# Moving a norm's sums to VectorE, a rescaling by one product, and a row broadcast's place in a two-block network on one core

## The chip, the cores and the metric

The kernel runs on one core of a Trainium2 chip. Its time is the device time of one execution in microseconds, the median of repeated runs. The core's engines work side by side and each takes its own instructions in the order in which the program lists them: PE (TensorE, matrix products; PEld is its weight load), DVE (VectorE), ACT (ScalarE), POOL (GpSimd) and SP, which here only issues DMAs. They wait for each other through semaphores.

## The reference

A sequence of 256 tokens with 1024 features passes two different blocks of two layers each; all is float32.

```
for i in range(2):                       # first block
    proj = rmsnorm(x, norm_mix[i]) @ w_in[i]
    q, k, v, cb, cc, cx, u, g = split(proj)
    y_attn = sliding_window_attention(rope(q), rope(k), v, sinks) @ w_attn_o[i]
    y_conv = (cb * short_conv(cc * cx, conv_w[i])) @ w_conv_o[i]
    ys = gelu(s5_ssm(u, ...));  y_ssm = (ys * sigmoid(ys @ w_ssm_glu[i])) @ w_ssm_o[i]
    x = x + (gated sum of y_attn, y_conv, y_ssm) @ w_mix_o[i]
    x = x + swiglu(rmsnorm(x, norm_ffn[i]))
x = rmsnorm(x, norm_final)
for l in range(2):                       # second block
    u = rmsnorm(h, norm_mix_w[l]) @ w_in[l]
    q, k, v, g_ret, z, xbc, dt, gate_ret, gate_ssd = split(u)
    yr = retention(rotary(q), rotary(k), v)            # 4 heads
    yr = silu(g_ret) * yr * rsqrt(mean(yr^2) + eps);   o_ret = yr @ ret_out
    xs, B, C = split(silu(conv(xbc)));  dtp = softplus(dt + dt_bias);  a = -exp(a_log)
    ys = (ssd_scan(xs * dtp, dtp * a, B, C) + d_skip * xs) * silu(z)
    ys = ys * rsqrt(mean over each of 4 groups(ys^2) + eps) * ssd_norm_w;  o_ssd = ys @ ssd_out
    h = h + (sigmoid(gate_ret) * o_ret + sigmoid(gate_ssd) * o_ssd) @ w_o
    h = h + swiglu(rmsnorm(h, norm_ffn_w[l]))
return rmsnorm(h, final_norm_w)
```

## The kernel before

Features lie on the 128 partitions and tokens along the free side: `X` holds x as 8 slices of 128 features by 256 tokens. Each product is done in three passes of fp32r matmuls: an operand is cut into a high part and the rest, and high times high, high times rest and rest times high are added. For the activations that pair is `xhl`. For weights `chunk` (line 264) does it as they stream in: a DMA on SP's queue fills `raw` (4 buffers of 128x1024), ACT copies it to `wh`, DVE subtracts to `wl` (5 buffers each). So a stream of DMA, ACT and DVE steps of one chunk each runs ahead of PE through the whole kernel. `fm` gives a product with features on the partitions, `tm` with tokens there, `fmb` is a two-pass form; `mid` hooks let other work in at half of a product. A scheduler orders each engine's instructions by the order of the code and by its own reckoning of when operands are ready; `tc.high_priority(offset=URGENT)` lets some go ahead, and `pinned` keeps a piece behind whatever its engines were given before it.

**Norms.** The scale of an rmsnorm is not known when the products that need it start. They run on `X` times the norm's gain, and the scale comes in later. While the last product of a layer ends, `Norm.pair(mp)` (line 426) makes the `xhl` of two slices and `squares(mp)` squares them on ACT into `sq` (2 buffers), and adds them into `acc`: on VectorE for the last pair and for the first norm of all, otherwise on GpSimd (line 444). `steps` sums `acc` over the partitions with four small matmuls into `st`, and takes a reciprocal square root of two columns on DVE (`rsqrt`, line 371: 15 or so tiny instructions). `rowbc` (line 398) makes a row of it for all partitions: two diagonal tiles `dg` on DVE, two small matmuls into `ax`, and a copy. `rescale` then overwrites `xhl` with the scaled values: four multiplications on POOL into `sq`, eight casts on ACT, eight subtractions on DVE.

**State space of the first block.** While layer 0 of the first block ends, and through its feed-forward, the kernel prepares the tables of layer 1's state-space model: steps A1 and A2 on POOL (powers and rotations, tiles `BP`, `W`, `g`), PC, CP, BX, WK, KK on the other engines, each pinned, in the order of `PLAN_1`.

**Retention (`layer2`).** For head 0 the products for q, k and v run on unscaled `xhl`. In the middle of v's product `mid_v` finishes the norm and rotates q and k with scaled tables; v is scaled as it leaves PSUM (line 1399), `nm.rescale()` follows (line 1402), and the product for the gate `sg` (line 1404, `silu2`) reads scaled `xhl`. Later heads need nothing of the kind. `head_tail` normalizes a head's result with `rd` (line 1355).

**State space of the second block.** Four groups follow, with three convolved products, two products for z and one gate each. What is left of a group, `group_tail` (line 1475), is a generator that `bg.tick()` moves on by one step after each product of the next group: two steps with the decay matrices, sums of squares in `acc`, one step for the next decay matrices, one with the small sum into `ax`, `rsqrt` and `dg`, one with the two matmuls on `dg` and the copy `rdb`, and a last one that makes the tiles `y`. `dt_prep` (line 1244) is run in steps between the four products with `ret_out`; it loads `a_log` into `al` and takes its exponential (line 1261).

Of the kernel before, what the change touches and what calls it, by code (L numbers as in the profile page):

```python
# [13 lines left out]
ALU = mybir.AluOpType  # L14
# [55 lines left out]
def body(ctx, tc, A, out):  # L70
# [29 lines left out]
    def axt(shape=(128, 2, 256)):  # L100
        return T(ax, list(shape), "ax")
# [7 lines left out]
    def add(o, a, b, eng=V):  # L109
        return tt(o, a, b, ALU.add, eng)  # L110
# [7 lines left out]
    def ts(o, a, s1, s2, op0, op1, eng=V):  # L118
        return eng.tensor_scalar(out=o, in0=a, scalar1=s1, scalar2=s2, op0=op0, op1=op1)

    def act(o, i, f, bias=None, scale=None, accum=None):
        kw = {}
        if bias is not None:
            kw["bias"] = bias
        if scale is not None:
            kw["scale"] = scale
        if accum is not None:
            kw["accum_out"] = accum
        return SC.activation(out=o, in_=i, func=f, **kw)  # L129
# [265 lines left out]
            stt(y, t, 1.5, src, ALU.add, ALU.mult)  # L395
        return y

    def rowbc(colv, o):

        dg = T(sqp, [128, 2, 128], "dg")  # L400
        with tc.high_priority(offset=URGENT):
            for b in range(2):
                ts(dg[:, b, :], ident, colv[:, b:b + 1], None, ALU.mult, ALU.bypass)
        yield
        ps = axt([128, 512])
        for b in range(2):
            mmu(ps[:, b * 128:b * 128 + 128], ones, dg[:, b, :], b == 0, b == 1)
        cp(o, ps[:, 0:S])
# [3 lines left out]
    class Norm:  # L412
# [24 lines left out]
        def squares(self, mp):  # L437
            sq = T(tmp, [128, 2, S], "sq")
            act(sq, X[:, 2 * mp:2 * mp + 2, :], AF.Square)
            if self.sqgain is not None:  # L440
                self.sums()
                self.todo = mp, sq
                return
            eng = V if mp == 3 or self.gain is gfirst else G
            if mp == 0:
                self.acc = T(sqp, [128, S], "acc")
                add(self.acc, sq[:, 0], sq[:, 1], eng)
            else:
                for k in range(2):
                    add(self.acc, self.acc, sq[:, k], eng)  # L450

        def sums(self):
            if self.todo is None:
# [766 lines left out]
        sub(o[:, 0, :], a[:, 0, :], b[:, 1, :])  # L1220
        add(o[:, 1, :], b[:, 0, :], a[:, 1, :])

    def silu2(ps, o):

        for b in range(2):
            act(o[:, b], ps[b], AF.Tanh, scale=0.5)
            stt(o[:, b], o[:, b], 1.0, ps[b], ALU.add, ALU.mult)

    def layer2(l, nm, nxt):
# [13 lines left out]
        def dt_prep():  # L1243
            pd = mmt()
            for k0, kn, (wh, wl) in chunks(w, 11264, D, n=32):
                for k in range(kn):
                    kt = k0 + k
                    mmu(pd[0:32, 0, :], wl[:, k, :], xh[:, kt, :], kt == 0, False)
                    mmu(pd[0:32, 0, :], wh[:, k, :], xl[:, kt, :], False, False)
                    mmu(pd[0:32, 0, :], wh[:, k, :], xh[:, kt, :], False, kt == D // 128 - 1)  # L1250
            acr = T(lp, [32, S], "acr")
            cp(acr, pd[0:32, 0, :])
            yield
            ps = axt()
            for b in range(2):
                PE.transpose(ps[:, b, 0:32], acr[:, 128 * b:128 * b + 128], ident[0:32, 0:32])
            dtb = T(lp, [128, 32], "dtb")
            nc.sync.dma_start(out=dtb, in_=A["dt_bias_2"][l].partition_broadcast(128))
            al = T(lp, [128, 32], "al")
            nc.sync.dma_start(out=al, in_=A["a_log_2"][l].partition_broadcast(128))  # L1260
            act(al, al, AF.Exp)
            x = T(lp, [128, 2, 32], "x")
            for b in range(2):
                add(x[:, b, :], ps[:, b, 0:32], dtb)
            e = T(lp, [128, 2, 32], "e")
            z_ = T(lp, [128, 2, 32], "z_")
            pl = T(lp, [128, 2, 32], "pl")
            stt(e, x, -1.0, x, ALU.mult, ALU.max)
            act(e, e, AF.Exp, scale=-1.0)
            ts(pl, e, 2.0, None, ALU.add, ALU.bypass)  # L1270
            V.reciprocal(out=pl, in_=pl)
            mul(e, e, pl)
            mul(z_, e, e)
            ts(pl, z_, 1.0 / 17.0, None, ALU.mult, ALU.bypass)
            for kk in range(7, 0, -1):
                stt(pl, pl, 1.0 / (2 * kk + 1), z_, ALU.add, ALU.mult)
            stt(pl, pl, 1.0, e, ALU.add, ALU.mult)
            ts(x, x, 0.0, None, ALU.max, ALU.bypass)
            dtp = T(lp, [128, 2, 32], "dtp")
            stt(dtp, pl, 2.0, x, ALU.mult, ALU.add)  # L1280
            la = T(lp, [128, 2, 32], "la")
            stt(la, dtp, -1.0, bc(al, 2), ALU.mult, ALU.mult)
            dth = T(lp, [128, 2, 32], "dth")
            ts(dth, dtp, 0.5, None, ALU.mult, ALU.bypass)
            yield
            pn = axt([128, 512])
            mmu(pn[:, 0:32], tri, la[:, 0, :], True, True)
            mmu(pn[:, 32:64], strict, la[:, 0, :], True, True)
            mmu(pn[:, 64:96], tri, la[:, 1, :], True, True)
            for b in range(2):  # L1290
                mmu(pn[0:32, 128 + 128 * b:256 + 128 * b], la[:, b, :], tri, True, True)
            ncol = T(lp, [128, 3, 32], "ncol")
            V.tensor_copy(out=ncol[:, 0, :], in_=pn[:, 0:32])
            ts(ncol[:, 1, :], pn[:, 32:64], -1.0, None, ALU.mult, ALU.bypass)
            V.tensor_copy(out=ncol[:, 2, :], in_=pn[:, 64:96])
            acr = T(lp, [32, S], "acr")
            cp(acr, pn[0:32, 128:384])
            acd = T(dramp, [32, S], f"acd{l}")
            nc.sync.dma_start(out=acd, in_=acr)
            sd.update(dth=dth, ncol=ncol, acd=acd)  # L1300
# [29 lines left out]
        def head_tail(h):  # L1330
            qT, kT, v, sg = (hd[h][k] for k in ("qT", "kT", "v", "sg"))
            dec = T(r1, [128, 384], "dec")
            nc.sync.dma_start(out=dec, in_=A["decay"][h])
            pst = axt([128, 512])
            for kk in range(2):
                mmu(pst[:, 0:256], kT[:, kk, 0:128], qT[:, kk, :], kk == 0, False)
            for kk in range(2):
                mmu(pst[:, 256:384], kT[:, kk, 128:256], qT[:, kk, 128:256], False, kk == 1)
            stt_ = T(r2, [128, 384], "st")
            mul(stt_, pst[:, 0:384], dec)  # L1340
            yield
            y3 = T(r2, [128, 2, 512], "y3")
            ss = T(sm, [128, 2], "ss")
            for b in range(2):
                py = axt([128, 512])
                if b == 0:
                    mmu(py, stt_[:, 0:128], v[:, 0, :], True, True)
                else:
                    mmu(py, stt_[:, 128:256], v[:, 0, :], True, False)
                    mmu(py, stt_[:, 256:384], v[:, 1, :], False, True)  # L1350
                sq = T(tmp, [128, 2, S], "sq").rearrange("p a s -> p (a s)")
                act(sq, py, AF.Square, accum=ss[:, b:b + 1])
                mul(y3[:, b], py, sg[:, b])
                yield
            rd = rsqrt(ss, 2, 1.0 / 512)
            ts(rd, rd, 0.5, None, ALU.mult, ALU.bypass)
            for b in range(2):
                ts(y3[:, b], y3[:, b], rd[:, b:b + 1], None, ALU.mult, ALU.bypass)
            yield
            for c in range(2):  # L1360
                pt = axt()
                for m in range(2):
                    for b in range(2):
                        k = (2 * c + m) * 128
                        PE.transpose(pt[:, m, 128 * b:128 * b + 128], y3[:, b, k:k + 128], ident)  # L1365
                t = pair(yp, "y")
                split(t, pt)
                yr[2 * h + c] = t
                yield

        for h in range(4):
# [26 lines left out]
            for b in range(2):  # L1398
                cp(v[:, b, :], ps[b], nm.rsc[:, b:b + 1] if h == 0 else None)
            bg.tick()  # L1400
            if h == 0:
                nm.rescale()
            sg = e["sg"] = T(r2, [128, 2, 512], "sg")
            silu2(tm(w, 4096 + 512 * h, D, XX, mid=bg.tick), sg)
            bg.tick()
            bg.add(head_tail(h))
            if h == 0 and nm.sqgain is not None:
# [66 lines left out]
        def group_tail(g):  # L1474
# [28 lines left out]
            ps = axt([128, 512])  # L1503
            for b in range(2):
                mmu(ps[:, b:b + 1], acc[:, b * 128:b * 128 + 128], ones[:, 0:1], True, True)
            rd = rsqrt(ps[:, 0:2], 2, 1.0 / 512)
            rdb = T(d1, [128, S], "rdb")
            yield from rowbc(rd, rdb)
            yield
            for c in range(2):  # L1510
                t = pair(yp, "y")
                mul(sz[c], sz[c], bc(rdb, 2))
# [139 lines left out]
```

## Time and profile before

| | |
|---|---|
| time, median of 3 runs | 2252.89 us (2251.32 to 2256.33) |
| the profiled execution's own time | 2256.99 us |
| its span, first to last instruction | 2255.2 us |
| busy PE / DVE / ACT / POOL | 97% / 69% / 54% / 9% of the span |
| mean granted clock of TensorE | 0.986 |
| moved from HBM | 386.88 MB, 175 GB/s over the span |

PE is busy nearly all the time and does the same matmuls whatever the order, so what can change is its idle time and the stretches in which it is granted half its clock. The waits in which PE stands idle are short and spread over the span, but for one of 16.94 us.

### The profile page before, as it was taken

The page shows a single profiled execution, that of the slowest core. Times are in us where ns is not written, and L with a number is a line of the kernel's source. Part 1 is how long each engine was busy: PE and PEld are TensorE (multiplying, and loading weights), DVE is VectorE, ACT ScalarE, POOL GpSimd, SP SyncE. Part 2 cuts the span into 40 slices and gives each one's busy share as a digit, 9 for nine tenths or more (in the row PEclk, how much of TensorE's full clock was granted, in tenths as well). Part 3 has the DMA queues.
Part 4 walks back from the last instruction along what each step waited for, and adds up shares of the span by engine and source line. Part 5 has one row for each costly group of instructions (what it writes and reads, how often), then busy time and mean ns, then how long its engine had stood idle before and what let it go on. Part 6 is the DMA issues. An engine that isn't in the chain of part 4 may idle for free. (4 is left out here: it accounts for less than half of the span.)

```text
span 2255.2 us, 36864 instructions
## 1 busy us (share of the span) xinstructions
PE 2178.6 (97%) x14368; PEld 1971.0 (87%) x14368; DVE 1548.2 (69%) x2515; ACT 1221.7 (54%) x1949; POOL 199.6 (9%) x359
## 2 busy tenths in 40 slices
PE   7999969999999999999999999999999999999997
PEld 6898958899999889888999989889888899989886
DVE  7766646568756655776568887556766668887554
ACT  6666537645555444444476755444444477655442
POOL 5810244001000000100000000000100000000000
PEclk9899989999999999999999999999999999999999
DMA  6443537766645655555566646555555566456553
GB/s 184 148 127 122 168 120 240 233 207 220 195 136 178 191 186 173 162 186 165 160 201 202 187 157 192 186 174 183 171 166 177 161 200 199 149 185 196 185 178 103
DMA packets 343935, 397.75 MB, mean 176 GB/s; under 512 B 27988, under 2 KB 276688, under 8 KB 342736
## 3 DMA queue, kind: packets, MB, share of 16 engines
q1 hardware_dynamic: 342816, 394.48, 56.0%
q8 instruction: 113, 1.85, 0.3%
q10 hardware_dynamic: 592, 0.79, 0.1%
q14 instruction: 62, 0.51, 0.1%
q0 software_dynamic: 352, 0.11, 0.0%
HBM read 386.88 MB, written 8.45 MB: 175 GB/s over the span
## 5 line engine op out<-in xcount | busy, mean ns | idle before, releaser
L104 DVE TENSOR_TENSOR wl<-raw,wh 128x1024 fp32r<-128x1024 f32 (+1 forms) x698 | 850.1, 1221 | 516.5 <-ACT wh L129 488.4
L129 ACT ACTIVATE wh<-raw 128x1024 fp32r<-128x1024 f32 (+1 forms) x698 | 727.8, 1047 | 822.5 <-PE mm L135 663.4
L135 PE MATMUL mm<-xhl,wh 128*128 128x256 f32 x3616 | 672.2, 287 | 4.9 <-ACT xhl L129 3.2
L135 PE MATMUL mm<-wh,xhl 128*128 128x512 f32 (+1 forms) x2176 | 645.3, 381 | 3.0 <-DVE xhl L116 1.3
L135 PEld LDWEIGHTS mm<-xhl,wh 128*128 128x128 f32 x3616 | 567.7, 192 | 11.5 <-ACT xhl L129 4.1
L135 PE MATMUL mm<-xhl,wl 128*128 128x256 f32 (+1 forms) x1808 | 515.3, 285 | 3.8 <-DVE wl L104 3.8
L135 PEld LDWEIGHTS mm<-wh,xhl 128*128 128x128 f32 x2176 | 398.7, 190 | 81.3 <-issue 4.3
L135 PE MATMUL mm<-wl,xhl 128*128 128x512 f32 (+1 forms) x1088 | 410.4, 377 | 5.5 <-DVE wl L104 5.5
L135 PEld LDWEIGHTS mm<-xhl,wl 128*128 128x128 f32 (+1 forms) x1808 | 347.6, 192 | 5.7 <-DVE wl L104 4.9
L135 PEld LDWEIGHTS mm<-wl,xhl 128*128 128x128 f32 x1088 | 206.8, 190 | 43.2 <-DVE wl L104 6.0
L135 PE MATMUL mm<-hh,wh 128*128 128x512 f32 (+1 forms) x660 | 185.4, 348 | 0.0
L135 PE MATMUL mm<-y,wh 128*128 128x512 f32 (+1 forms) x576 | 182.1, 372 | 1.0 <-DVE y L116 1.0
L135 PE MATMUL mm<-hh,wl 128*128 128x256 f32 x528 | 147.9, 280 | 0.0
L135 PE MATMUL mm<-y,wl 128*128 128x256 f32 x512 | 144.3, 282 | 0.0
L135 PEld LDWEIGHTS mm<-hh,wh 128*128 128x128 f32 x660 | 114.7, 188 | 16.7
L135 PEld LDWEIGHTS mm<-y,wh 128*128 128x128 f32 x576 | 103.8, 188 | 21.9 <-DVE y L116 1.7
L104 POOL TENSOR_TENSOR acc<-sq 128x256 f32<-128x256 f32 x6 | 4.8, 795 | 1245.3 <-ACT sq L129 1245.3
L135 PEld LDWEIGHTS mm<-hh,wl 128*128 128x128 f32 x528 | 99.1, 188 | 0.0
L135 PEld LDWEIGHTS mm<-y,wl 128*128 128x128 f32 x512 | 96.2, 188 | 0.5 <-issue 0.3
L135 PE MATMUL mm<-mg,wh 128*128 128x256 f32 x512 | 90.5, 280 | 0.0
L135 PEld LDWEIGHTS mm<-mg,wh 128*128 128x128 f32 x512 | 78.4, 189 | 0.0
L116 DVE SCALAR_TENSOR_TENSOR ta<-mm,vec,ta 128x255 f32<-128x255 f32 (+2 forms) x144 | 67.2, 476 | 9.5 <-ACT ta L129 9.2
(363 smaller groups left out, 2446.6 us busy)
## 6 DMA issues: line engine op xcount, KB each, us to landing
raw<-in_w_in_dram SPq DMA_DIRECT2D x284, 512.0 KB, 4.3
raw<-in_w_ffn_in_dram SPq DMA_DIRECT2D x88, 512.0 KB, 3.6
raw<-in_w_gate_up_dram SPq DMA_DIRECT2D x88, 512.0 KB, 3.5
raw<-in_w_down_dram SPq DMA_DIRECT2D x42, 512.0 KB, 3.8
raw<-in_w_ffn_out_dram SPq DMA_DIRECT2D x40, 512.0 KB, 3.5
raw<-in_ret_out_dram SPq DMA_DIRECT2D x32, 512.0 KB, 3.8
raw<-in_ssd_out_dram SPq DMA_DIRECT2D x32, 512.0 KB, 3.4
raw<-in_w_mix_o_dram SPq DMA_DIRECT2D x16, 512.0 KB, 3.4
```

Of the source, the lines that this page charges most:

```text
L104: return eng.tensor_tensor(out=o, in0=a, in1=b, op=op)
L116: return V.scalar_tensor_tensor(out=o, in0=a, scalar=s, in1=b, op0=op0, op1=op1)
L129: return SC.activation(out=o, in_=i, func=f, **kw)
L135: return PE.matmul(out=o, lhsT=l, rhs=r, start=start, stop=stop)
```

## The change

Three edits go together, with a pin for one exponential:

- `Norm.squares` adds all squares on VectorE; GpSimd has no part in sums any more.
- In head 0 of the retention the product for the gate runs on unscaled `xhl`. Its tanh takes the scale as an operand (`rh`, half of `nm.rsc`), the factor that is still missing in front comes in with `rd` in `head_tail`, and `nm.rescale()` is called behind the product.
- In the state-space norm `rsqrt` gets priority; `rowbc` gives back control once more between `dg` and its matmuls, and the step behind the copy goes.
- The exponential of `al` is pinned behind what ACT was given before.

```
-            eng = V if mp == 3 or self.gain is gfirst else G
             if mp == 0:
                 self.acc = T(sqp, [128, S], "acc")
-                add(self.acc, sq[:, 0], sq[:, 1], eng)
+                add(self.acc, sq[:, 0], sq[:, 1])
             else:
                 for k in range(2):
-                    add(self.acc, self.acc, sq[:, k], eng)
+                    add(self.acc, self.acc, sq[:, k])
...
-    def rowbc(colv, o):
+    def rowbc(colv, o, wait=False):
...
         yield
+        if wait:
+            yield
         ps = axt([128, 512])
...
-    def silu2(ps, o):
+    def silu2(ps, o, r=None):
         for b in range(2):
-            act(o[:, b], ps[b], AF.Tanh, scale=0.5)
+            act(o[:, b], ps[b], AF.Tanh, scale=0.5 if r is None else r[:, b:b + 1])
...
-            act(al, al, AF.Exp)
+            pinned(lambda: act(al, al, AF.Exp))
...
-            ts(rd, rd, 0.5, None, ALU.mult, ALU.bypass)
+            if h == 0:
+                stt(rd, rd, 0.5, nm.rsc, ALU.mult, ALU.mult)
+            else:
+                ts(rd, rd, 0.5, None, ALU.mult, ALU.bypass)
...
+            sg = e["sg"] = T(r2, [128, 2, 512], "sg")
+            pg = tm(w, 4096 + 512 * h, D, XX, mid=bg.tick)
             if h == 0:
+                rh = T(sm, [128, 2], "r8")
+                ts(rh, nm.rsc, 0.5, None, ALU.mult, ALU.bypass)
+                silu2(pg, sg, rh)
                 nm.rescale()
-            sg = e["sg"] = T(r2, [128, 2, 512], "sg")
-            silu2(tm(w, 4096 + 512 * h, D, XX, mid=bg.tick), sg)
+            else:
+                silu2(pg, sg)
...
-            rd = rsqrt(ps[:, 0:2], 2, 1.0 / 512)
+            with tc.high_priority(offset=URGENT):
+                rd = rsqrt(ps[:, 0:2], 2, 1.0 / 512)
             rdb = T(d1, [128, S], "rdb")
-            yield from rowbc(rd, rdb)
-            yield
+            yield from rowbc(rd, rdb, True)
```

The scheduler decides what stands where. The first place is VectorE at the end of layer 0's mixer, where `acc_3315` is the sum of the feed-forward norm's squares and `wl` are rests of weight chunks:

```order
 L116 SCALAR_TENSOR_TENSOR xhl_92<-X,vec,xhl_92 128x256 x2
+L104 TENSOR_TENSOR acc_3315<-sq_3313 128x256
 L104 TENSOR_TENSOR wl_3490<-raw_3488,wh_3489 128x1024
 L116 SCALAR_TENSOR_TENSOR X<-mm_3317,X 128x512
 L104 TENSOR_TENSOR wl_3561<-raw_3559,wh_3560 128x1024
 L116 SCALAR_TENSOR_TENSOR xhl_92<-X,vec,xhl_92 128x256 x2
+L104 TENSOR_TENSOR acc_3315<-acc_3315,sq_3383 128x256 x2
 L104 TENSOR_TENSOR wl_3579<-raw_3577,wh_3578 128x1024
 L116 SCALAR_TENSOR_TENSOR X<-mm_3387,X 128x512
 L104 TENSOR_TENSOR wl_3649<-raw_3647,wh_3648 128x1024
 L116 SCALAR_TENSOR_TENSOR xhl_92<-X,vec,xhl_92 128x256 x2
+L104 TENSOR_TENSOR acc_3315<-acc_3315,sq_3453 128x256 x2
```

The five adds of the first three pairs now stand on VectorE right behind the `xhl` of their pair; on POOL they stood between state-space steps. The last pair's two adds stay where they were.

The second place is ScalarE at head 0 of the last layer's retention, from the copy of the norm's row (`rsb`) on; `xhl` from `sq` are the casts of `rescale`. Before:

```order
L129 ACTIVATE rsb_17035<-ax_17077 128x256
L129 ACTIVATE xhl_92<-sq_17133,vec 128x256 x2
L129 ACTIVATE xhl_92<-sq_17139,vec 128x256 x2
L129 ACTIVATE wh_17215<-raw_17214 128x1024
L129 ACTIVATE v_16890<-mm_17039,rsc_17016 128x512
L129 ACTIVATE wh_17241<-raw_17240 128x1024
L129 ACTIVATE v_16890<-mm_17040,rsc_17016 128x512
L129 ACTIVATE xhl_92<-sq_17145,vec 128x256 x2
L129 ACTIVATE xhl_92<-sq_17151,vec 128x256 x2
```

And now:

```order
L129 ACTIVATE rsb_17037<-ax_17079 128x256
L129 ACTIVATE wh_17193<-raw_17192 128x1024
L129 ACTIVATE v_16892<-mm_17041,rsc_17018 128x512
L129 ACTIVATE wh_17245<-raw_17244 128x1024
L129 ACTIVATE v_16892<-mm_17042,rsc_17018 128x512
L129 ACTIVATE xhl_92<-sq_17216,vec 128x256
L129 ACTIVATE wh_17275<-raw_17274 128x1024
L129 ACTIVATE xhl_92<-sq_17216,vec 128x256
L129 ACTIVATE xhl_92<-sq_17222,vec 128x256
L129 ACTIVATE wh_17321<-raw_17320 128x1024
L129 ACTIVATE xhl_92<-sq_17222,vec 128x256
L129 ACTIVATE xhl_92<-sq_17228,vec 128x256
```

The casts stand one or two at a time between weight chunks, behind v's two copies; four of them stood ahead of those copies. The last two stand among the gate's tanh.

The third place is PE in the second block's state space, at the tail of the third group in layer 0; `dg` is the diagonal of its norm, `mm_14500` the first product with `ssd_out`. Before:

```order
L135 MATMUL mm_14348<-xhl_92,wl_14381 128x256
L135 MATMUL mm_14500<-y_13319,wh_14503 128x512
...
L135 MATMUL mm_14501<-y_13319,wh_14503 128x512
L135 MATMUL ax_14330<-dg_14264,C 128x128 x2
L1471 MATMUL ax_14335<-C,xs_2239_13886 128x128 x2
```

And now, where the gate's product is `mm_14346` and the product with `ssd_out` `mm_14502`:

```order
L135 MATMUL mm_14346<-xhl_92,wl_14379 128x256
L135 MATMUL ax_14408<-dg_14266,C 128x128 x2
L135 MATMUL ax_14425<-Lm_14143,xd_14332 64x256 x2
...
L135 MATMUL ax_14440<-Lm_14159,xd_14332 64x128 x2
L135 MATMUL mm_14502<-y_13321,wh_14505 128x512
```

Nine matmuls on `y` that stood ahead of `dg`'s now stand behind it, and the eight transposes of `xs` moved from behind `dg`'s matmuls to the start of the gate's product. In the first and second group `dg`'s matmuls stand three matmuls of the gate's product earlier than before.

## Rows read from the trace of the kernel before

**Rows 1.** The page: busy time, share of the span and instructions.

```profile
PE 2178.6 (97%) x14368; PEld 1971.0 (87%) x14368; DVE 1548.2 (69%) x2515; ACT 1221.7 (54%) x1949; POOL 199.6 (9%) x359
```

**Rows 2.** Waits of PE over the span: who waits for whom, total us, times, longest.

```profile
PE st L135 <- DVE acc L104: 16.9, 1, 16.9
...
PE ax L135 <- DVE dg L119: 8.3, 5, 3.2
...
PE mm L135 <- ACT xhl L129: 3.2, 2, 2.6
```

**Rows 3.** Timeline of PE: start, us, instruction, count, [idle before, what ended it].

```profile
307.12 1.01 PE L135 MATMUL st<-C,acc 128*128 128x1 f32 x4 [16.94 <-DVE acc L104]
...
1320.02 0.71 PE L135 MATMUL ax<-dg,C 128*128 128x128 f32 x4 [1.26 <-DVE dg L119]
...
1588.28 0.50 PE L135 MATMUL mm<-xhl,wh 128*128 128x256 f32 x2 [2.57 <-ACT xhl L129]
...
1607.86 0.47 PE L135 MATMUL mm<-wh,xhl 128*128 128x512 f32 x1 [0.43 <-DVE tb L104]
1608.74 0.49 PE L135 MATMUL mm<-wh,xhl 128*128 128x512 f32 x1 [0.41 <-ACT v L129]
1610.02 0.50 PE L135 MATMUL mm<-wh,xhl 128*128 128x512 f32 x1 [0.79 <-DVE xhl L116]
```

**Rows 4.** Timeline of POOL: a norm's last adds, and the last layer's rescaling.

```profile
304.62 1.52 POOL L104 TENSOR_TENSOR acc<-acc,sq 128x256 f32<-128x256 f32 x2
...
1602.78 3.45 POOL L104 TENSOR_TENSOR sq<-X,rsb 128x512 f32<-128x512 f32 x2 [29.18 <-issue]
```

**Rows 5.** Timeline of DVE at the end of layer 0's mixer.

```profile
281.26 0.87 DVE L116 SCALAR_TENSOR_TENSOR xhl<-X,vec,xhl 128x256 fp32r<-128x256 f32 x2
...
286.95 1.59 DVE L116 SCALAR_TENSOR_TENSOR xhl<-X,vec,xhl 128x256 fp32r<-128x256 f32 x2
306.18 0.89 DVE L104 TENSOR_TENSOR acc<-acc,sq 128x256 f32<-128x256 f32 x2 [17.64 <-POOL acc L104]
```

**Rows 6.** Stretches: us, busy PE, PEld, DVE, ACT, POOL, then clock, DMA share, GB/s.

```profile
307.10:313.25 6.15, 6.13 (x16) 4.98 (x17) 4.83 (x19) 0.13 (x1) 0.00 (x0) 0.50 0.54 167
...
952.00:958.00 6.00, 6.00 (x20) 4.75 (x20) 6.00 (x10) 2.01 (x5) 3.55 (x2) 0.72 0.16 47
...
1610.00:1616.00 6.00, 5.98 (x19) 4.79 (x20) 6.00 (x9) 1.94 (x6) 3.54 (x2) 0.72 0.13 30
...
1938.00:1942.00 4.00, 3.41 (x17) 3.42 (x17) 3.53 (x8) 1.40 (x4) 0.00 (x0) 0.57 0.85 260
...
1208.00:1236.00 28.00, 26.98 (x228) 26.41 (x225) 25.39 (x51) 23.61 (x44) 0.00 (x0) 1.00 0.56 165
```

**Rows 7.** Instructions on `acc`: count, min/median/max ns, first and last start.

```profile
L104 DVE TENSOR_TENSOR acc<-acc,sq x34: 411/418/427, 17.3 to 2057.6; 128x256 f32<-128x256 f32 x34
...
L104 POOL TENSOR_TENSOR acc<-acc,sq x24: 721/762/804, 291.3 to 2051.9; 128x256 f32<-128x256 f32 x24
```

**Rows 8.** Timeline of ACT: a square, `al`, and v in the last layer.

```profile
293.32 0.63 ACT L129 ACTIVATE sq<-X 128x512 f32<-128x512 f32 x1 [6.81 <-POOL acc L104]
...
1586.65 0.23 ACT L129 ACTIVATE al<-al 128x32 f32<-128x32 f32 x1 [4.34 <-DMA al<-in_a_log_dram]
...
1608.03 0.67 ACT L129 ACTIVATE v<-mm,rsc 128x512 f32<-128x512 f32 x1
```

**Rows 9.** Timeline of DVE: last layer's first norm and rescaling, second group's `dg`.

```profile
1583.80 0.68 DVE L104 TENSOR_TENSOR X<-X,ta 128x512 f32<-128x512 f32 x1
...
1613.91 2.71 DVE L116 SCALAR_TENSOR_TENSOR xhl<-sq,vec,xhl 128x256 fp32r<-128x256 f32 x4
...
1936.52 1.23 DVE L104 TENSOR_TENSOR wl<-raw,wh 128x1024 fp32r<-128x1024 f32 x1 [2.06 <-ACT wh L129]
...
1938.24 0.48 DVE L119 TENSOR_SCALAR dg<-C,ny 128x128 f32<-128x128 f32 x2
```

## Prediction

> **What bounds the kernel now.** I read the page's busy times first: PE is busy 97% of the span [rows 1], and the change leaves its matmuls as they are. So time can come only from PE's idle stretches and from stretches at half clock, and next come PE's waits, grouped by who ends them [rows 2]. One stands out: the statistics product `st` waits 16.9 us, once, for `acc` on VectorE. The waits for `dg` come to 8.3 us in five, and those for casts of `xhl` to 3.2 us in two. The timeline of PE then says where each lies [rows 3]; the timelines of POOL, DVE and ACT [rows 4, 5, 8, 9] say what was late, and the windows [rows 6] what the clock did afterwards. VectorE has 31% of its span free [rows 1], so extra adds there cost nothing by themselves; they cost only where PE waits for what stands behind them.
>
> **Sums on VectorE.** In the feed-forward norm of the first layer, PE is ready for `st` at 307.12 − 16.94 = 290.18. VectorE's last two adds stand idle for 17.64 us and end that wait [rows 5]; they follow POOL's two adds of 304.62, which end at 306.14 [rows 4]. Those are nothing in themselves (762 ns each, [rows 7]): they stand behind state-space steps in POOL's queue. ACT's last square was held too, 6.81 us for a buffer of `sq` [rows 8]; without that it is done at 293.32 − 6.81 + 0.63 = 287.1. In the changed kernel the adds of the first three pairs follow their `xhl` on VectorE, and the last two follow the `xhl` pair that ends at 286.95 + 1.59 = 288.54 [rows 5]. At 418 ns each [rows 7] that is 289.4, before PE's 290.18. The stall goes, and so does its aftermath: for 6.15 us behind it the granted clock is 0.50 [rows 6], the lower level, which costs 3.1 us. 16.9 + 3.1 = 20.0.
>
> Against it: that `xhl` pair took 1.59 us where the one before took 0.87 [rows 5], at a time when POOL was in its state-space steps. If the two adds are stretched as the pair was (1.83 times), they end at 290.1; if each is held a whole 0.8 us (one POOL add), at 291.0, and `st` waits 0.8 us, with as much again for what stands before. I take 0.5 us lost: **19.5** (18.4 to 20.0).
>
> The Trainium skill ("SBUF — State Buffer", section "Who interferes with whom") says that a VectorE instruction with two SBUF inputs contends with a GpSimd instruction that reads SBUF, and that the loser blocks fully. An `acc` add is such an instruction, so the rule speaks against moving adds to an engine beside a busy POOL; the 1.59 against 0.87 us agree with it. By it the term would be its lower end, 18.4, since each add can lose one POOL instruction and no more.
>
> Thirty adds move. 24 of them show as POOL's [rows 7], and 30 × 0.418 = 12.5 us of VectorE work is hidden by its idle time. At the other norms' ends no wait of PE on POOL's adds shows beside the one of 16.9 [rows 2], so nothing is gained there; where cover is gone a norm's end may cost up to 1.6 us, as above. POOL's state-space steps only come earlier.
>
> **The rescale, one product later.** In the last layer's head 0 PE has three gaps near the end of v's product: 0.43 for the tables `tb`, 0.41 for `v`, 0.79 for `xhl` [rows 3], in all 1.63; the other layer has 0.2 less. Behind them the clock averages 0.72 over 6 us in either layer [rows 6], which is 3.4 us at half clock, or 1.7 lost. Now the gate's product reads unscaled `xhl`: its 0.79 goes. v's copies (0.67, [rows 8]) stand ahead of all casts, where four stood before them, so I take the 0.41 as gone; the 0.43 for `tb` stays, since the tables come from the same norm chain. That leaves 1.2 of gaps, cut to 1.0 for the smaller layer and the tables' jitter. The clock falls after the three gaps together; with one left I give its return 0.7, 1.2 of 1.7. **2.2 a layer, 4.4 in all.** What is late next is the rescaling's end: POOL's `sq` takes 3.45 [rows 4], and VectorE's last four `xhl` end at 1616.62 [rows 9], 13.8 us behind the first multiplication. It now has to overwrite `xhl` behind the last reading matmul of the gate's product, and head 1's q product reads it next. But the overwriting goes by slices and can follow the gate's last pass slice by slice, and that product comes to its last slices some 3.6 us in (a quarter of a three-pass product at the pace seen here). From below: if 5 us of the chain show in the two layers together, the term is −0.6; if more, it is the last rival. Bounds −0.6 to 6.4 (all gaps and all the clock).
>
> **`al` pinned.** In the last layer ACT stands 4.34 us for the DMA of `al`, and its casts and weight copies stand behind; PE's first product waits 2.57 us for `xhl` [rows 8, 3]. X is ready at 1584.48 [rows 9], before al's 1586.65, so the cast had only ACT to wait for. Pinned behind what was given before, the exponential stands near `dt_prep`'s others, its data long there. **2.4** (0 to 2.57, since another link may be late by a few tenths).
>
> **The state-space norm's row.** PE waits for `dg` five times over 0.2 us, 8.3 in all, 3.2 the longest [rows 2]; 1.26 at 1320.02 is the third group of the first of the two layers [rows 3]. In groups one and two `dg` still stands behind the same `wl` on VectorE, which is 25.39 of 28 us busy there [rows 6], so it hardly comes earlier: at 1936.52 a `wl` starts late behind ACT, ends 1937.75, and `dg` starts at 1938.24 [rows 9], 0.49 that `rsqrt`'s last small instructions take. With priority these go ahead of that `wl`. But PE's `dg` matmuls come three matmuls, some 0.36 us (at 28/228, [rows 6]), earlier too. Net 0.2 to 0.9 a place, I take 0.5: 2.0 at four. The 4 us at clock 0.57 behind the long wait [rows 6] are 3.4 us at half, 1.7 lost, of which I credit 0.7: 1.2. In the third group `dg` stands two `wl` earlier, and nine matmuls on `y` that stood ahead now follow as cover at the tail: 0.7 and 0.5. **4.4.** Bounds: if PE's earlier arrival eats everything, −1; if all 8.3 and 1.7 go, and the tail's 0.5 with them, 10.5.
>
> **The sum.** 19.5 + 4.4 + 2.4 + 4.4 = 30.7. The profiled execution took 2256.99, 4.1 above the median of the runs; 2256.99 − 30.7 = 2226.3, and as a median 2226.3 − 4.1 = **2222.2**.
>
> **Rivals.**
> - *The `dg` waits stay.* Everything that `rsqrt` gains is lost to the earlier matmuls, because VectorE's queue of `wl` sets both. For it: 25.39 of 28 us busy. Against: the longest wait began behind ACT, not behind that queue. 2222.2 + 4.4 = 2226.6; 0.12.
> - *The adds on VectorE make waits of their own.* At six norm ends (those not already summed there) up to 1.6 us shows, since `xhl` and weight rests stand behind the adds. For it: the stretched pair. Against: VectorE is 31% idle. 2222.2 + 6 × 1.6 = 2231.8; 0.10.
> - *All `dg` waits go.* The term is 10.5 to 11, the time 2215.7; 0.11.
> - *The rescaling shows whole* (the other side). If POOL's multiplications, the casts and the rests cannot start before the gate's product has been read through, head 1's q product waits for the chain of 13.8 us in either layer: 27.7, and with clock loss as behind the 16.94 stall, 3.1 each, 33.8; the 4.4 of that edit is lost as well. 2222.2 + 33.8 + 4.4 = 2260.4, 0.3% slower. It decides from the point where more than 1616.62 − 1602.78 − 3.6 = 10.2 us of the chain lie behind the gate's last matmul. For it: one buffer `xhl` is read and overwritten. Against: writes go by slices, and four of the eight casts stood between v's matmuls before without harm but 0.79. 0.03.
> - *The change doesn't do what it says:* the 16.9 us come from something other than POOL's adds, ACT's square or the last `xhl`, and half of the stall stays: 2232. 0.02.
>
> **How the numbers follow.** My forecast has 0.62, with its own range 2217 to 2228. To hold eight in ten I take in the ends with dear adds and with all `dg` waits gone: **2212 to 2236**. This kernel's measurement tells about 0.2%, 4.5 us, from no change. Only the rescaling rival ends above 2257, so slower has 0.03; between 2248 and 2257 some 9 to 18 of 30.7 us would have to be lost beyond the rivals above, 0.02; faster has 0.95.
>
> **What would show it.** In the changed kernel's profile: no `st` wait for `acc` above 1 us, no `acc` rows on POOL, and a granted clock of 1.00 from 285 to 310; no gap near 1588 for `xhl`, and `al` much later on ACT; before the gate's product at most one gap, and full clock behind it; a sum of waits for `dg` of 4 to 6 us. It is wrong if head 1's q product waits for `xhl` by more than a microsecond, if feed-forward products of any norm newly wait for `acc`, or if the 20 us come back as a wait for the state-space tables of the next layer.

## The result and the profile after

The changed kernel takes 2225.34 us (median of 4 runs, 2222.40 to 2227.24), the kernel before 2254.61 (4 runs): 29.3 us less, a ratio of 0.987, 95% interval 0.9852 to 0.9889. The forecast was 2222.2, which is 30.7 us below 2252.89, the median of the kernel before that was known then. The profiled execution of the changed kernel took 2224.35, with a span of 2222.6; the mean granted clock is 0.989.

First the page's busy times, and the grouped waits of PE (total us, times, longest), as in [rows 1, 2].

```profile
PE 2171.8 (98%) x14368; PEld 1966.6 (88%) x14368; DVE 1553.1 (70%) x2547; ACT 1221.3 (55%) x1949; POOL 183.7 (8%) x329
```

```profile
PE ax L135 <- DVE dg L119: 3.1, 5, 1.8
PE mm L135 <- ACT xhl L129: 2.5, 1, 2.5
PE mm L135 <- DVE xhl L116: 1.1, 2, 0.8
```

The row of `st` is gone, that of `dg` fell from 8.3 to 3.1, and the 2.5 for casts is one wait at the start of the program. `xhl` from VectorE is still there, but its two waits are others (below). PE is busy 6.8 us less with the same matmuls: that is clock, and the rest of the gain is idle time.

Then the places of the prediction on the timeline of PE (start, us, instruction, count, idle before and what ended it):

```profile
291.81 0.50 PE L135 MATMUL st<-C,acc 128*128 128x1 f32 x4
...
1256.84 0.71 PE L135 MATMUL ax<-dg,C 128*128 128x128 f32 x4 [1.78 <-DVE dg L119]
...
1583.84 0.70 PE L135 MATMUL mm<-wh,xhl 128*128 128x512 f32 x2 [0.43 <-DVE tb L104]
...
1599.85 0.39 PE L135 MATMUL mm<-xhl,wh 128*128 128x256 f32 x1 [0.80 <-DVE xhl L116]
```

Against [rows 3]: `st` has no idle time ahead of it (16.94 before). Of the three gaps near the end of v's product the one for `tb` is left. The gap of 0.79 for `xhl` is no longer there, but one of 0.80 stands 16 us later, in head 1's q product, behind the rescaling's last rest. The gap of 2.57 at 1588 has no successor; `al` now runs at 1764.9 in that layer.

The windows answer to [rows 6] (us, busy PE, PEld, DVE, ACT, POOL, then clock, DMA share, GB/s): full clock behind the norm and around the gate's product, and half clock left at the second group's `dg` of the first of the two layers.

```profile
285.00:310.00 25.00, 25.00 (x124) 21.04 (x123) 23.56 (x39) 12.91 (x20) 23.68 (x42) 1.00 0.57 174
931.00:937.00 6.00, 5.67 (x25) 4.72 (x26) 6.00 (x11) 3.77 (x7) 0.00 (x0) 1.00 0.28 87
1584.00:1604.00 20.00, 19.20 (x114) 17.00 (x113) 18.80 (x26) 11.38 (x18) 3.87 (x2) 1.00 0.59 183
...
1257.00:1261.00 4.00, 4.00 (x22) 4.00 (x23) 2.62 (x4) 2.08 (x4) 0.00 (x0) 0.57 0.96 302
```

Where the time came from can be read by following one matmul after another through both timelines:

| PE reaches | before | after | difference |
|---|---|---|---|
| first product after attention, layer 0 of the first block | 231.88 | 233.73 | +1.9 |
| `ax<-U,W` of its layer 1 | 520.94 | 502.60 | −18.3 |
| the wait for `tb`, layer 0 of the second block | 949.57 | 931.33 | −18.2 |
| `ax<-BC` of that layer | 1174.16 | 1153.43 | −20.7 |
| the wait for `tb`, last layer | 1607.86 | 1583.84 | −24.0 |
| `ax<-BC` of the last layer | 1833.07 | 1806.35 | −26.7 |
| last matmul's end | 2243.93 | 2211.30 | −32.6 |

These are single executions, 32.6 us apart, so the steps add up to more than the 29.3 between the medians. The stretch of the sums gave 20.2, the gate's product 2.5 and 2.7, `al` and the first layer's `dg` 3.3 together, the last layer's tails 5.9. The first 1.9 are not the change's: up to there every engine runs the same instructions in the same order in both kernels, and what differs is PE's idle time (28.1 us against 26.8) and the granted clock (0.93 against 0.95).

### The profile page after: what moved, and what is told of

Its sections match the earlier page's. It is cut to its first block, busy times and chain, and to the rows that moved or that the text cites. A ratio compares the mean times of both kernels' runs of the same rounds, so it can differ in the third digit from the quotient of the medians.

```text
span 2222.6 us, 36844 instructions
## 1 busy us (share of the span) xinstructions
PE 2171.8 (98%) x14368; PEld 1966.6 (88%) x14368; DVE 1553.1 (70%) x2547; ACT 1221.3 (55%) x1949; POOL 183.7 (8%) x329
## 4 chain that ended last, share of the span: by engine, by line
PE 78%; ACT 5%; DMA 4%; DVE 4%; issue 1%; SPq 0%; POOL 0%; ACTq 0%; DVEq 0%; POOLq 0%
PE mm L135 71%; PE ax L135 5%; ACT Lm L129 2%; DMA raw<-in_w_in_dram 2%; DMA Lm<-acd 2%; ACT wh L129 1%; DVE wl L104 1%; PE ax L567 1%; ACT ta L129 0%; DVE Lm L104 0%; PE ax L1369 0%; ACT tb L129 0%; PE st L135 0%; PE ax L1480 0%; DVE ta L116 0%
## 5 line engine op out<-in xcount | busy, mean ns | idle before, releaser
L104 POOL TENSOR_TENSOR sq<-X,rsb 128x512 f32<-128x512 f32 x12 | 21.8, 1823 | 1196.0 <-ACT rsb L129 1168.6
```

The source lines that it names most:

```text
L104: return eng.tensor_tensor(out=o, in0=a, in1=b, op=op)
```

## Experiments

Each ran beside the kernel before on the same chip. Gains are worked out from the ratio and the time of before there (2256 us for the first eight), not from the two medians. The first four make one edit each on the kernel before.

**The sums alone.**

```
-            eng = V if mp == 3 or self.gain is gfirst else G
...
-                    add(self.acc, self.acc, sq[:, k], eng)
+                    add(self.acc, self.acc, sq[:, k])
```

> Only the squares' adds go to VectorE; everything else as before. Theory: the stall of 16.9 us is POOL's queue and goes whole, with the half clock behind it: 20 us, so about 2234.5 against 2254.6; the wait of st for acc under 1 us, and all that stands behind that point earlier by the same 20 us to the end of the program (within 1 us), since 12.5 us of adds on VectorE are covered everywhere else. Rival: the adds on VectorE cost at the other norms' ends; then the lead of 20 us shrinks by 1 to 1.6 us at each of up to six places, and the time is 2240 or more.

Measured: 2233.54 against 2255.98, ratio 0.9909 (0.9891 to 0.9926), 20.5 us (17 to 25). `st` starts at 292.70 with no idle time. Between the first product after attention and `ax<-U,W` this trace has 268.9 us, the changed kernel's 268.9, that of the kernel before 289.1, and no other norm's end shows a new wait for `acc`. The rival falls: the adds are covered everywhere else.

**The gate's product alone** (the part of the diff on `silu2`, `rh`, `rd` and `rescale`).

> Only the rescaling one product later in the second block. Theory: 2.5 us a layer, so 5 us, about 2249.6 against 2254.6; of the three gaps near the end of v's product the first, 0.43 for tb, stays and the other two go; the granted clock stays at 1.00 there; a gap of 0.3 to 0.8 for xhl comes back in head 1's q product. Rival: the chain of the rescaling shows at head 1's q product in full, over 5 us a layer, and the time is above 2254.6.

Measured: 2249.44, ratio 0.9981 (0.9967 to 0.9995), 4.3 us (1 to 7). The gaps for `v` and `xhl` are gone in both layers, that for `tb` stays, and head 1's q product waits 0.33 and 0.81 for `xhl`. The gain agrees with the theory's 5 us; of the rescaling's chain the last microsecond shows, not its 13.8.

**The norm's row alone** (`rsqrt`'s priority, the extra step, the last step taken away).

> Only the state-space norm's row: priority for its rsqrt, dg's matmuls a step later. Theory: 6.5 us, about 2248, of it 6 in the last layer (the wait of 3.2 with its half clock goes) and below 1 in the first (the second group's 1.8 stays). Rival 1: the first forecast, 4.4 us, 2250.2, with 0.5 at each place. Rival 2: this edit gains nothing by itself, and the last layer's gain in the changed kernel came from where the weight stream stood after the other edits; then 2254 and the wait of about 3 us stays.

Measured: 2249.69, ratio 0.9977 (0.9964 to 0.9991), 5.2 us (2 to 8). The waits for `dg` sum to 5.2. But the last layer's second group still waits 3.11: the long wait, whose end I had put down to this edit after reading the trace, stayed. Neither the theory's split nor the forecast's holds.

**`al` alone.**

> Only the exponential of al pinned. Theory: PE's gap of 2.57 us for xhl at the start of the last layer goes and nothing else moves: 2252.0 against 2254.6, just beyond what a measurement tells; in the trace everything behind that point is 2.5 us earlier. Rival: the weight copies, which stood behind al too, are late by another link, and the gap shrinks by 1 us or less.

Measured: 2251.36, ratio 0.9984 (0.9971 to 0.9996), 3.6 us (0.9 to 6.5), and the gap is gone. In the eight traces of kernels without this edit it is 1.2 to 2.6 us, so 2.57 was at the upper end.

**One pair's adds instead of three.** As before, but `eng = V if mp >= 2 ...`.

> As before, but the two adds of the third pair of slices go to VectorE; the three adds of the first two pairs stay on POOL, where the last of them ended at 293.3 in the trace of before. Theory (a place in POOL's queue, not the engine that adds): the stall of 17 us at st becomes one of 293.3 + 4 x 0.42 - 290.2 = 4.8 us, with the half clock behind it for 3.4 to 6.8 us; 12 to 14 us gained, 2242 to 2244. Rival (VectorE's speed is what counts, five adds of 0.76 us against 0.42): two adds of five moved give a small part, 1 to 2 us, and the wait stays over 12 us.

Measured: 2242.35, ratio 0.9944 (0.9929 to 0.9959), 12.6 us (9 to 16). The rival falls: two adds of five moved give three fifths. The wait is 7.72, though, not 4.8. VectorE's and POOL's timelines show why:

```profile
290.88 1.69 DVE L104 TENSOR_TENSOR acc<-acc,sq 128x256 f32<-128x256 f32 x2 [9.55 <-POOL acc L104]
292.50 1.21 DVE L104 TENSOR_TENSOR wl<-raw,wh 128x1024 fp32r<-128x1024 f32 x1
293.63 0.68 DVE L116 SCALAR_TENSOR_TENSOR X<-mm,X 128x512 f32<-128x512 f32 x1
...
295.36 0.87 DVE L116 SCALAR_TENSOR_TENSOR xhl<-X,vec,xhl 128x256 fp32r<-128x256 f32 x2
296.15 0.88 DVE L104 TENSOR_TENSOR acc<-acc,sq 128x256 f32<-128x256 f32 x2
```

```profile
290.13 0.72 POOL L104 TENSOR_TENSOR acc<-acc,sq 128x256 f32<-128x256 f32 x1
```

The third pair's adds now wait on VectorE for POOL's, 9.55 us, and hold up all behind them: a weight rest, the last `X`, its `xhl`, and only then the last two adds. My expectation had counted the adds alone.

**The two halves of the row.** With `rsqrt`'s priority only:

```
+            with tc.high_priority(offset=URGENT):
+                rd = rsqrt(ps[:, 0:2], 2, 1.0 / 512)
```

> Only the priority of rsqrt in the state-space norm. Theory: rsqrt's small instructions move up, but dg stays behind a rest of a weight chunk, so the six waits for dg still sum to 6 to 8 us and the time is that of before, 2255 (less than 2 us gained). Rival: the priority is what gains in the edit of the row; then the waits for dg sum to 4 to 5.5 us, and it is 2250 to 2252.

Measured: 2254.19, ratio 1.0000 (0.9987 to 1.0013); the waits for `dg` sum to 7.3. Its VectorE and PE in the last layer's second group show why nothing comes of it: the small instructions are done 1.8 us ahead of the rest `wl`, which waits for ACT's copy of its chunk, and `dg` stands behind that rest:

```profile
1937.12 0.16 DVE L116 SCALAR_TENSOR_TENSOR ny<-nt,ny 128x2 f32<-128x2 f32 x1
1939.04 1.23 DVE L104 TENSOR_TENSOR wl<-raw,wh 128x1024 fp32r<-128x1024 f32 x1 [1.77 <-ACT wh L129]
1940.18 0.48 DVE L119 TENSOR_SCALAR dg<-C,ny 128x128 f32<-128x128 f32 x2
```

```profile
1940.52 0.98 PE L135 MATMUL ax<-dg,C 128*128 128x128 f32 x4 [3.04 <-DVE dg L119]
```

With the step only (`rowbc(rd, rdb, True)` and the last `yield` removed):

> Only the extra step between dg and its matmuls, with the last step taken away. Theory: the third group's waits and those for y at the first product with ssd_out go (1 to 1.3 a layer), the second group's stay; 2 to 3 us gained, 2253. Rival: the matmuls' later place is what gains in the edit of the row, 5 to 6 us, and the sum of the waits for dg falls to 5 us.

Measured: 2251.90, ratio 0.9985 (0.9974 to 0.9996), 3.4 us (0.9 to 5.9). The third group's waits are gone in both layers, the second group's are 2.1 and 3.7, and against the theory the waits for `y` stay, 0.5 a layer. The trace is of the slowest of twelve executions (2256.01), and its waits for `dg` sum to 7.7, so it does not show where the 3.4 come from. By the times the step gains, and the priority shows no gain by itself (2.9 us at most by its interval); whether priority adds to the step (5.2 against 3.4) the intervals leave open.

**The kernel before once more.**

> The kernel before once more, word for word, for a second trace of it. Theory: the waits for dg hang on how late the weight stream's DMA is just there, so single ones move by 1 to 3 us from run to run (the one of 3.2 us may be 0.7 to 3.5), while the stall at st is 17 to 18 us again and the gaps at v's product are the same within 0.1. Rival: the program fixes these waits, and 1.0, 1.8, 1.3, 1.1, 3.2 and 0.1 come back within 0.3.

Measured: 2255.75. Its waits of PE (columns as above), and the last layer's second group on the timeline of PE:

```profile
PE st L135 <- DVE acc L104: 18.2, 1, 18.2
PE ax L135 <- DVE dg L119: 4.9, 6, 1.6
```

```profile
1939.25 0.71 PE L135 MATMUL ax<-dg,C 128*128 128x128 f32 x4 [1.32 <-DVE dg L119]
```

The same program waits 4.9 us for `dg` in one execution and 8.3 [rows 2] in another; 3.21 became 1.32. The stall at `st` and the gaps of 0.4 to 0.8 at v's product come back. The rival falls.

**The changed kernel once more, and three variants of it.** `dgpool` makes `dg` on POOL, `castfirst` swaps two lines, `both` does both:

```
+                ts(dg[:, b, :], ident, colv[:, b:b + 1], None, ALU.mult, ALU.bypass, G if wait else V)
...
-                silu2(pg, sg, rh)
                 nm.rescale()
+                silu2(pg, sg, rh)
```

> The changed kernel once more, word for word, for a second trace and a time beside the next three. Theory: 2225 again, within 3; no wait of st; the waits for dg 2 to 5.5 us in all instead of 3.1, since they hang on the weight stream of the moment; the gaps for xhl at head 1's q product 0.3 and 0.8 again, since they hang on the order alone.

> The changed kernel, with dg of the state-space norm made on POOL, whose queue is empty there, instead of VectorE behind a rest of a weight chunk. Theory (dg's place behind a late weight rest makes the long waits): no wait for dg over 1.2 us is left; short ones grow to 0.5 to 1.0, since POOL takes 0.76 where VectorE takes 0.42 for an add and two dg take 0.5 on VectorE; 0 to 2 us gained, 2223 to 2225, less than a measurement tells, so the trace decides. Rival (rsqrt's last instructions are late, not dg): the second groups' waits stay at 1 to 3 us.

> The changed kernel, with the rescaling called ahead of the gate's tanh, so that the last cast and the last rest of xhl stand one instruction of 0.67 us earlier on ScalarE and VectorE. Theory: head 1's q product waits for just that last rest, so its gaps fall from 0.33 and 0.80 to 0 and 0.2; 0.9 us in all, below what a measurement tells: 2224 to 2225. Rival: the gap is set by POOL's multiplications, which wait for their buffers, and stays at 0.8.

> The changed kernel with both edits, dg on POOL and the rescaling called ahead of the tanh. Theory: 1 to 3 us below the changed kernel, 2222 to 2224. Rival: no gain, since what dg no longer waits for comes back as a wait for xd or for weight rests: 2225.

Measured, against 2253.63 of the kernel before:

| | us | ratio | waits for `dg`, sum | for `xhl` at head 1's q |
|---|---|---|---|---|
| changed kernel again | 2223.36 | 0.9867 (0.9847 to 0.9888) | 3.1 | 0.30, 0.75 |
| `dgpool` | 2231.17 | 0.9898 (0.9882 to 0.9913) | 8.8 | 0.30, 0.75 |
| `castfirst` | 2222.24 | 0.9851 (0.9831 to 0.9871) | 5.4 | under 0.1, 0.18 |
| `both` | 2226.34 | 0.9879 (0.9861 to 0.9896) | 8.8 | under 0.1, 0.18 |

`castfirst` does what its theory says to the gap; its time is the lowest of all, but not told apart from the changed kernel's. `dgpool` is slower than the changed kernel beside it, 7 us by the ratios, whose intervals barely meet; that is the opposite of its theory, and the longest wait for `dg` is 1.9. `both` shows no gain over the changed kernel either, and is 6 us behind `castfirst`, again with `dg` on POOL and waits of 8.8. Its instructions on `dg` (count, ns min/median/max, first and last start), and the longest pair on the timeline of POOL with VectorE's beside it:

```profile
L119 DVE TENSOR_SCALAR dg<-C,rsc x16: 279/286/1581, 29.8 to 2041.1; 128x128 f32<-128x128 f32 x16
L119 POOL TENSOR_SCALAR dg<-C,ny x16: 595/605/3710, 1213.5 to 1974.0; 128x128 f32<-128x128 f32 x16
```

```profile
1297.14 4.29 POOL L119 TENSOR_SCALAR dg<-C,ny 128x128 f32<-128x128 f32 x2 [38.74 <-DVE ny L116]
```

```profile
1296.82 0.15 DVE L116 SCALAR_TENSOR_TENSOR ny<-nt,ny 128x2 f32<-128x2 f32 x1
1296.89 3.49 DVE L104 TENSOR_TENSOR wl<-raw,wh 128x1024 fp32r<-128x1024 f32 x3
```

POOL had nothing queued and started when `ny` was there, yet its first `dg` took 3.71 us and ended 0.5 us behind the run of three weight rests on VectorE (1300.38). The same came back in both layers of `dgpool` and of `both`: four first `dg` of a third group, each beside three rests, each 3709 or 3710 ns. The wait for a place in VectorE's queue became a wait for VectorE itself.

In `castfirst` the last layer's second group waits 2.97 for `dg`, and its timelines of VectorE and ACT show the cause:

```profile
1900.71 0.15 DVE L116 SCALAR_TENSOR_TENSOR ny<-nt,ny 128x2 f32<-128x2 f32 x1
1902.60 1.22 DVE L104 TENSOR_TENSOR wl<-raw,wh 128x1024 fp32r<-128x1024 f32 x1 [1.74 <-ACT wh L129]
1903.74 0.48 DVE L119 TENSOR_SCALAR dg<-C,ny 128x128 f32<-128x128 f32 x2
```

```profile
1901.51 1.06 ACT L129 ACTIVATE wh<-raw 128x1024 fp32r<-128x1024 f32 x1 [2.50 <-DMA raw<-in_w_in_dram]
```

With priority the norm's last small instruction ends at 1900.86, and `dg` still starts at 1903.74: it stands behind a weight rest whose chunk came late from HBM. In `prio` and in `row` ACT's copy there waits for the DMA in the same way (2.55 and 2.88), and in the changed kernel's wait of 1.78 with less (1.40). In the kernel before `dg` stands behind a late rest too [rows 9], but its trace puts ACT's wait there down to a matmul; that the DMA held it is not shown.

## Why the prediction was right, and where not

- **The sums** (forecast 19.5, measured 20.5 alone and 20.2 by the table). The working held step by step. In the changed kernel the last `xhl` pair and the last adds run beside POOL's tables, and the adds are stretched as in the estimate, to 1.59 us; PE comes to `st` only 0.5 us after their end, so the 0.5 taken off was not lost. The 20 us did not come back at the next layer's tables: `ax<-U,W` has a wait of 1.19 there, 1.18 before. The two timelines, with POOL's third:

```profile
288.81 1.00 DVE L116 SCALAR_TENSOR_TENSOR xhl<-X,vec,xhl 128x256 fp32r<-128x256 f32 x2
289.74 1.59 DVE L104 TENSOR_TENSOR acc<-acc,sq 128x256 f32<-128x256 f32 x2
```

```profile
289.61 1.44 POOL L104 TENSOR_TENSOR g<-W,s_rot 128x256 f32<-128x256 f32 x2
```

  That the stall was POOL's order and not its speed is shown by `third`: POOL kept three of the five adds, and three fifths of the gain came. The 1.59 us stand against 0.89 that two adds took with POOL done [rows 5]. The rule of the Trainium skill cited above ("SBUF — State Buffer", "Who interferes with whom") agrees with that. The cost was there, but it stayed within its cover.
- **The rescale** (forecast 4.4, measured 4.3 alone, 2.5 and 2.7 by the table). Two of three gaps went in either layer. The clock's share was a chance: over the eight traces without this edit it fell near v's product in 8 of 16 places (6 of the 8 in the last layer), over the six with it in none of 12. So on average about half of the 1.7 was there to be had, 0.9 a layer by estimate, not the 1.2 that I took. A gap of 0.3 and 0.8 came back at head 1's q product; each is under the microsecond that the prediction had set as its limit, but the 4.4 had no term for them. `castfirst` shows that the last cast's and rest's place behind the gate's tanh sets it.
- **`al`** (forecast 2.4, measured 3.6 alone, 0.9 to 6.5). The gap went whole; its size before varies from 1.2 to 2.6.
- **The row** (forecast 4.4, measured 5.2 alone, 2 to 8). The sum lies within that, but the step behind most of it failed, so the agreement is luck in part: "With priority these go ahead of that `wl`... Net 0.2 to 0.9 a place". They do go ahead, and that shows no gain by itself, since `dg` stays behind that rest and the rest waits for a late chunk. The third group's cover, of which I took 0.7 and 0.5, is not shown to be what gained: the step alone gives 3.4, and the third group has no wait in the five traces with it (`dg` on VectorE), but without it those waits vary from none to 1.7, and `third` has none either. With both halves the waits for `y` at the first product with `ssd_out` are gone in all six traces; with either half alone they stay, 0.5 a layer. And the 5.9 us that the table shows in the last layer are partly chance: without the edit the waits for `dg` sum to 4.9 to 9.3 in a trace (six traces, counting neither half of the row), with it to 3.1 to 5.4 (four, `dg` on VectorE); the changed kernel's 3.1 is below the 4 to 6 that I had named. What priority adds beyond the waits for `y` stays open.
- **The rivals.** Waits for `dg` that stay, adds that make waits of their own, and a rescaling that shows whole did not come; nor did all waits for `dg` go. One sum of the chances is wrong: 2248 and 2257 lie 25.8 and 34.8 us above the forecast, and 12 and 21 above the 2236 at which the range ends, not 9 to 18. Nothing else hangs on it.

## What to carry to other kernels

A long wait for a trivial instruction asks for its neighbours in the queue, not for its duration: five adds of 0.76 us cost 20 us of the end, clock included, since they stood between unrelated work on an engine that takes its instructions in order. When moving part of such a chain to another engine, move all of it: what is left behind holds up the new queue too. And before crediting an edit with a wait that went, look at a second trace of the unedited kernel; waits behind a weight stream moved by 2 us here with no edit at all.

## What the runs showed of the hardware

An idle engine was not a free one: the same 128x128 multiplication that makes `dg` took 286 ns (median) on VectorE and 605 on POOL, and up to 3710 there while VectorE ran weight rests with two inputs in SBUF. The Trainium skill ("SBUF — State Buffer", "Who interferes with whom") states that VectorE with two SBUF inputs contends with a GpSimd instruction that reads SBUF, and calls the shared port pair an exclusive lock. The 3710 ns beside three rests of 3.49 us together agree, and go further than one instruction: in all four places the multiplication ended only behind the third rest.
